# Five edits to a fused two-layer decoder trunk: order of the softmax division, of a weight load, of three scheduled steps, and a weight sum by accumulating transfer

## The chip, the cores and the metric

The kernel runs on one core of a Trainium2 chip. The metric is device microseconds per execution; the kernel before has a median of 2035.91 us in three runs. The engines are TensorE (PE; its weight loads are shown as PEld), VectorE (DVE), ScalarE (ACT), GpSimd (POOL) and SyncE (SP), which here only issues transfers.

## The reference

A trunk of two layers on 256 tokens of width 2048, float32. Layer 0 mixes by gated linear attention (4 heads, chunks of 64 tokens), layer 1 by sliding-window attention with a sink per head (32 query heads, 4 key/value heads, window 128). Each layer ends with a squared-ReLU MLP of width 8192.

```
u = rmsnorm(h, norm_mix[layer])
h = h + gla_mixer(u, ...)            # layer 0: gates from rank-16 product glr @ w_g2
k_band, v_band = shared_kv(h, ...)   # once, after layer 0
h = h + swa_sink_mixer(u, ...)       # layer 1
h = h + sqrelu_mlp(rmsnorm(h, norm_mlp[layer]), w1, w2)
```

In the attention the scores are masked, a softmax with the sink as a further column is taken (`p = softmax(concat([s, sink]))[..., :-1]`), and `o = p @ v`.

## The kernel before

Every float32 weight is read once from HBM in blocks of 512 x 512 (1 MB, tile `ws`, three buffers) and split by `halve`: ScalarE casts it to a high part `wh` (line 114), VectorE subtracts to get the low part `wl` (line 115), in two halves of 128 x 1024 each. The operands are split likewise, and each product is high x high, high x low and low x high. TensorE accumulates in eight banks: two "tp" (transposes), two "ms" and four "acc".

**What sets the order.** Each engine's list is fixed when the kernel is built. Work beside the main products is put off by `later(n, fn)`, due n ticks on, a tick being a quarter or half of a product's matmuls. `high_priority` lets the loads and splits (`WPRI`) and a few small steps (`QPRI`) be taken earlier in an engine's list than where they stand in the code; `issue_after` puts an instruction behind another one. SP issues the weight loads in order, each when its buffer is free.

**Start.** `first_piece` (lines 383, 401, 402) loads x and the first weight in four steps c = 0 to 3, each in six transfers of 256 KB. `glr` (lines 512, 517, 518) then makes the gates' rank from one 1 MB load.

**Gated attention.** `levels(hp, n)` schedules, for a pair of heads hp, the diagonal gram after 4 ticks (lines 601 to 614 in `diag`), and seven levels of decay grams, the first after n ticks and one each two ticks; `CS` is 14. Each level's operands are made by VectorE, GpSimd and ScalarE (lines 584 to 590, tile `mlev`, two buffers), its grams go to an "ms" bank.

**Residual.** `add_to` adds a finished 512-wide column block c to the stream (line 847) and schedules `operands`, which transposes it back (line 831) and scales it for the next product (lines 339, 340). `last` is 2 in both residuals that have room for Strassen-like products, and c = 3 is finished first there.

**MLP, second weight.** `seven` multiplies 1024 x 1024 blocks with seven products (a Strassen-like scheme), for each quarter g of the hidden width and each half n of the output. `product("A", 0, x)` takes a block `x` from the stream; `more(x, 0, 1)` adds a second block to it in SBUF by an accumulating transfer, issued by POOL (line 1004); `y`'s second block `b12` is loaded to `ws` and added by VectorE (line 1088, 128 x 2048). The summed `y` is used by `product("C", 6, y)`, the summed `x` by `product("D", 4, x)`.

**Sliding-window attention.** For each of four head groups g, beside the query product of the next group, `attend` schedules for the two token blocks t: scores and softmax (`a`), `divide` (lines 1291 to 1293), `masked` and `weighted`; `ATT` gives the ticks of t = 0 and t = 1, so that t = 1 goes first in each. `masked` transposes the divided weights for two halves f (line 1302) into "tp" banks; for t = 1 VectorE multiplies them by two masks into `po` and `pv` (line 1310), for t = 0 ScalarE copies them (line 1305). `weighted` multiplies by the values (vv), 64 columns for each f, f = 0 to partitions 0 to 63 of one "ms" bank and f = 1 to 64 to 127.

Of the kernel before, what the change touches and what calls it, by code (L numbers as in the profile page):

```python
# [8 lines left out]
F32 = mybir.dt.float32  # L9
# [7 lines left out]
P = 128  # L17
# [3 lines left out]
KT = D // P  # L21
# [12 lines left out]
WS = 3  # L34
WHL = 4
WPRI = 60
QPRI = 100
LV = 2
WARM = 11
CS = 14  # L40
# [9 lines left out]
def yoco_kernel(ctx: ExitStack, tc: tile.TileContext, x, norms, mlp_w1, mlp_w2, a_w_in, w_glr, w_gate, a_g_o, a_w_o,  # L50
                kv_w_k, kv_w_v, kv_g_k, b_w_q, b_g_q, b_sinks, b_w_o, out):
    nc = tc.nc
# [4 lines left out]
    wp = ctx.enter_context(tc.tile_pool(name="wp", bufs=2))  # L57
# [14 lines left out]
    def later(n, fn):  # L72
        due.setdefault(now[0] + n, []).append(fn)
# [141 lines left out]
    class Seven:  # L215
# [16 lines left out]
        def load(self, i, j):  # L232
            ws = wp.tile([P, 4, C], F32, name="ws", tag="ws", bufs=WS)
            with tc.high_priority(offset=WPRI):
                nc.sync.dma_start(out=ws, in_=self.block(i, j))
            return ws
# [42 lines left out]
        def run(self, after, order="1 21 3 7 31 e 5 20 30 6 2 4"):  # L279

            for step in order.split():
                if len(step) == 2:
                    i, j = int(step[0]), int(step[1])
                    self.plain(i, j, *("EF" if j else "AC"))
                else:
                    (self.ef if step == "e" else getattr(self, "p" + step))(after)
# [178 lines left out]
    def rstd_x():  # L465
        for c in range(NC4):
            later(2 + c // 2, lambda c=c: square_x(c))
        later(5, sum_x)
        later(9, norm_x)
        later(10, lambda: along(rb, rstd))  # L470
        later(10, lambda: nc.scalar.mul(out=rbq, in_=rb, mul=DK ** -0.5))
# [29 lines left out]
    def load_gate():  # L501
# [2 lines left out]
        nc.scalar.copy(out=wgh, in_=wg)  # L504
        nc.vector.tensor_sub(out=wgl, in0=wg, in1=wgh.bitcast(F32))

    def glr(acc, n):


        ws = wp.tile([P, KT, P], F32, name="ws", tag="ws", bufs=WS)  # L510
        with tc.high_priority(offset=WPRI):
            nc.sync.dma_start(out=ws, in_=w_glr.rearrange("(k p) n -> p k n", p=P))
        for j in range(2):
            js = slice(8 * j, 8 * j + 8)
            wh = wp.tile([P, 8, P], F32R, name="wh", tag="wh", bufs=WHL)
            with tc.high_priority(offset=WPRI):
                nc.scalar.copy(out=wh, in_=ws[:, js])
                nc.vector.tensor_sub(out=wh[:, :, 64:96], in0=ws[:, js, 64:96], in1=wh.bitcast(F32)[:, :, 64:96])  # L518
            for k in range(8):
                kt = 8 * j + k  # L520
                mm(acc.rearrange("p u t -> p (u t)"), wh[:, k],
                   act0[kt // 4][2][:, kt % 4].rearrange("p u t -> p (u t)"), kt == 0, kt == KT - 1)
                if kt % 4 == 3:
                    tick()

        def evac():
            z = g2.tile([P, T], F32, name="z", tag="og")
            nc.scalar.copy(out=z, in_=acc[:, 1])
            nc.vector.tensor_add(out=z, in0=acc[:, 0], in1=z)
            nc.vector.tensor_mul(out=z, in0=z, in1=rb)  # L530
            nc.gpsimd.memset(z[96:128], 1.0)
            nc.scalar.copy(out=zin, in_=z)
            nc.vector.tensor_sub(out=zin[32:64], in0=z[32:64], in1=zin.bitcast(F32)[32:64])

        later(n, evac)
# [115 lines left out]
    def levels(hp, n):  # L651
        later(4, lambda: diag(hp))
        for i, s in enumerate(LEVELS):
            later(n + 2 * i, lambda s=s: level(s, hp))
        later(n + 2 * len(LEVELS), lambda: cross(hp))

    run = gemm_k(0, first=first_piece)
    for c in range(NC4):
        if c == NC4 - 1:
            rstd_x()  # L660
        run(c)
    later(3, load_gate)
    glr(bank([P, 2, T], "tp"), 5)
# [3 lines left out]
    for c2 in range(4):  # L667
        later(CS + c2, lambda c2=c2: cumsum(c2))
    go_all(gemm_q(0))
    levels(0, CS - 6)  # L670
    go_all(gemm_k(1))
    go_all(gemm_q(1))
    levels(1, 1)
# [161 lines left out]
    def operands(acts, gains, c, b):  # L835
        tp = back(c, b)
        for a, g in zip(acts, gains):
            if b == 0:
                a[c] = new_act()
            for j in range(2):  # L840
                kt = 2 * b + j
                scaled(a[c], kt, tp[:, j], g[:, c * 4 + kt:c * 4 + kt + 1])

    def add_to(c, acts, gains, sq, r, last=NC4 - 1):

        def evac(t, acc):
            nc.vector.tensor_add(out=xs[c][:, t], in0=acc, in1=xs[c][:, t])
            if not gains:
                return
            junk = sm.tile([P, C], F32, name="junk", tag="junk", bufs=1)  # L850
            nc.scalar.activation(out=junk, in_=xs[c][:, t], func=AF.Square, accum_out=sq[:, t, c:c + 1])
            if t == 0:
                for b in range(2):
                    later(1 + b, lambda b=b: operands(acts, gains, c, b))
                if c == last:
                    later(1, lambda: rstd_of(r, sq))
        return evac
# [81 lines left out]
    def mlp(w1, w2, act, r, gains):  # L939
# [46 lines left out]
        def seven(w, n, op, us, g, acts, gains, sq, nr):  # L986
# [9 lines left out]
            def load(pool, tag, bufs, i, j):  # L996
                ws = pool.tile([P, 4, C], F32, name=tag, tag=tag, bufs=bufs)
                with tc.high_priority(offset=WPRI):
                    nc.sync.dma_start(out=ws, in_=block(i, j).rearrange("(k p) n -> p k n", p=P))
                return ws  # L1000

            def more(ws, i, j):
                with tc.high_priority(offset=WPRI):
                    nc.gpsimd.dma_start(out=ws, in_=block(i, j).rearrange("(k p) n -> p k n", p=P), accum_op=ALU.add)  # L1004
# [9 lines left out]
            def product(b, o, ws):  # L1014
                p, st = use(b)
                halves = halve(ws)
                for k in range(4):
                    wh, wl = halves[k]
                    mm(p, op[o][:, 0, k], wh, st and k == 0, False, skip_group_check=True)
                    mm(p, op[o][:, 0, k], wl, False, False, skip_group_check=True)  # L1020
                    mm(p, op[o][:, 1, k], wh, False, k == 3, skip_group_check=True)
                tick()
                return p
# [43 lines left out]
                    later(1, lambda: rstd_of(nr, sq))  # L1067


            x = load(mp, "wx", 2, 0, 0)  # L1070
            p = product("A", 0, x)
            more(x, 0, 1)
            if g == 0:
                nc.scalar.mul(out=v, in_=p, mul=-1.0)
            else:
                sub(v, p)
            plain(2, 1, "E", "F")
            y = load(mp, "wy", 1, 1, 1)
            product("E", 2, y)
            plain(3, 1, "E", "F")  # L1080
            add(x12, banks["E"])
            add(x22, banks["F"])
            p = product("D", 4, x)
            more(x, 1, 1)
            add(x21, p)
            b12 = load(wp, "ws", WS, 0, 1)
            with tc.high_priority(offset=WPRI):
                nc.vector.tensor_add(out=y, in0=y, in1=b12)
            sub(x22, product("C", 6, y))
            for i in (2, 3):  # L1090
                plain(i, 0, "A", "C", i == 2)
# [101 lines left out]
    def rows(m, n):  # L1193
        return m.rearrange("p (o n) -> p o n", o=1).broadcast_to([P, n, P])
# [90 lines left out]
        nc.scalar.activation(out=es, in_=es, func=AF.Exp)  # L1285
        return es, su, rd

    def divide(sc, st):
        es, su, rd = st
        with tc.high_priority(offset=QPRI):  # L1290
            nc.vector.tensor_add(out=rd, in0=su, in1=es)
            nc.vector.reciprocal(out=rd, in_=rd)
            nc.vector.tensor_mul(out=sc, in0=sc, in1=rd.rearrange("p (b o) -> p b o", o=1).broadcast_to([P, 8, P]))  # L1293

    def masked(t, sc):

        scp = sc.rearrange("p (a f) n -> p f a n", f=2)
        pos = []
        for f in range(2):
            tp = bank([P, 4, P], "tp")  # L1300
            for p in range(4):
                nc.tensor.transpose(out=tp[:, p, :], in_=scp[:, f, p], identity=ident)
            po = s2.tile([P, 4, P], F32, name="po", tag="po")
            if t == 0:
                nc.scalar.copy(out=po, in_=tp)
                pos.append(((po, 0),))
            else:
                pv = s2.tile([P, 4, P], F32, name="pv", tag="pv")
                for o, m in ((po, ownT), (pv, prevT)):
                    nc.vector.tensor_mul(out=o, in0=tp, in1=rows(m, 4))  # L1310
                pos.append(((po, 1), (pv, 0)))
        return pos

# [12 lines left out]

    def attend(g):

        sc, sums, pos = {}, {}, {}

        def a(t):
            sc[t] = s2.tile([P, 8, P], F32, name="sc", tag="sc")
            scores(g, t, sc[t])
            sums[t] = softmax(g, t, sc[t])

        def b(t):
            pos[t] = masked(t, sc[t])

        for t in range(NT):
            steps = (lambda t=t: a(t), lambda t=t: divide(sc[t], sums[t]), lambda t=t: b(t),  # L1340
                     lambda t=t: weighted(g, t, pos[t]))
            for n, step in zip(ATT, steps):
                later(n[t], step)
# [56 lines left out]
```

## Time and profile before

| | us |
|---|---|
| median of three runs (lowest, highest) | 2035.91 (2034.97, 2035.98) |
| profiled execution, own time | 2036.59 |
| its span | 2034.9 |
| TensorE busy | 2023.3 (99%) |
| VectorE busy | 1546.8 (76%) |
| ScalarE busy | 1202.9 (59%) |
| GpSimd busy | 161.4 (8%) |
| mean granted TensorE clock | 1.00 |

A line of the timeline gives the start (us from the span's start), the duration, engine, source line, operation, output and inputs with shapes, how many such instructions in a row, and in brackets how long the engine had been idle and what ended that. A line of the waits gives the waiting engine's output and line, what it waited for, the total, the count and the longest, in us. Matmuls are pipelined: a record is longer than the distance to the next one, and busy time counts overlapping records once.

### The profile page before, as it was taken

To read this page: it belongs to the slowest core of one execution; us is meant where nothing else is said; L and a number is where in the kernel's file an instruction comes from. 1 tells how busy PE (TensorE), PEld (TensorE's weight loads), DVE (VectorE), ACT (ScalarE), POOL (GpSimd) and SP (SyncE) were. 2 spreads that over 40 slices of the span, in tenths; PEclk is the share of its full clock that TensorE was granted. 3 is DMA by queue.
4 is the path that set the end of the run, shared out by engine and by line. 5 is a ranking of instruction groups with operands and counts; after the bars stand their busy time and mean duration, and the time that the engine had idled before them with its cause. 6 is when DMAs were issued, how large, how long until landed. Compare 5 with 4: busy or idle time off the path is not lost.

```text
span 2034.9 us, 26993 instructions
## 1 busy us (share of the span) xinstructions
PE 2023.3 (99%) x10578; PEld 1716.3 (84%) x10578; DVE 1546.8 (76%) x1796; ACT 1202.9 (59%) x1638; POOL 161.4 (8%) x175
## 2 busy tenths in 40 slices
PE   9999999999999999999999999999999999999999
PEld 9988888888888888888887877788888888888887
DVE  6698787867866876786798676876876786787777
ACT  6746666656555655555566677655655555555555
POOL 2151110000000000000001121000000000000000
PEclk9999999999999999999999999999999999999999
DMA  8445876676965785776666543775785786687575
GB/s 287 160 140 179 224 207 207 188 255 179 267 229 190 225 267 186 213 242 228 186 207 188 166 145 123 200 258 186 227 264 191 200 255 218 188 255 230 186 224 148
DMA packets 219280, 423.15 MB, mean 208 GB/s; under 512 B 7328, under 2 KB 17840, under 8 KB 219152
## 3 DMA queue, kind: packets, MB, share of 16 engines
q1 hardware_dynamic: 194224, 376.59, 54.3%
q0 software_dynamic: 21568, 42.81, 12.2%
q10 hardware_dynamic: 3360, 2.01, 0.3%
q8 instruction: 83, 1.36, 0.3%
q14 instruction: 45, 0.37, 0.1%
HBM read 419.29 MB, written 2.10 MB: 207 GB/s over the span
## 4 chain that ended last, share of the span: by engine, by line
PE 91%; DVE 4%; ACT 2%; DMA 1%; issue 1%; POOL 0%; SPq 0%; ACTq 0%; DVEq 0%; POOLq 0%
PE acc L81 58%; PE ms L81 22%; PE tp L81 10%; DVE wl L115 1%; ACT sc L1283 1%; DMA ws<-in_a_w_in_dram 1%; DMA wx<-in_mlp_w_dram 1%; PE tp L831 0%; ACT wh L114 0%; DVE sc L1293 0%; PE tp L1215 0%; DVE st L1277 0%; DVE act L340 0%; PE tp L701 0%; DVE po L1310 0%
## 5 line engine op out<-in xcount | busy, mean ns | idle before, releaser
L115 DVE TENSOR_TENSOR wl<-ws,wh 128x1024 fp32r<-128x1024 f32 x600 | 737.7, 1238 | 277.9 <-ACT wh L114 274.6
L114 ACT CAST wh<-ws 128x1024 fp32r<-128x1024 f32 x600 | 629.0, 1052 | 448.9 <-PE acc L81 285.9
L81 PE MATMUL acc<-wh,act 128*128 128x512 f32 x1696 | 544.5, 394 | 0.5 <-DVE xs L1042 0.3
L81 PE MATMUL acc<-act,wh 128*128 128x512 f32 (+1 forms) x1536 | 453.7, 359 | 0.0
L81 PEld LDWEIGHTS acc<-wh,act 128*128 128x128 f32 x1696 | 317.5, 188 | 69.0 <-issue 2.0
L81 PE MATMUL acc<-act,wl 128*128 128x256 f32 x1280 | 355.1, 279 | 0.1
L81 PE MATMUL acc<-wl,act 128*128 128x512 f32 x848 | 330.2, 390 | 0.0
L81 PEld LDWEIGHTS acc<-act,wh 128*128 128x128 f32 x1536 | 272.6, 189 | 43.5
L115 DVE TENSOR_TENSOR wl<-wx,wh 128x1024 fp32r<-128x1024 f32 x160 | 193.5, 1222 | 87.6 <-ACT wh L114 85.2
L114 ACT CAST wh<-wx 128x1024 fp32r<-128x1024 f32 x160 | 167.9, 1054 | 143.4 <-PE acc L81 81.1
L81 PEld LDWEIGHTS acc<-act,wl 128*128 128x128 f32 x1280 | 241.3, 189 | 1.6 <-DVE wl L402 0.3
L81 PE MATMUL tp<-act,wh 128*128 128x512 f32 x528 | 204.6, 392 | 0.8 <-DVE wh L518 0.8
L81 PE MATMUL ms<-act,wh 128*128 128x512 f32 x512 | 202.0, 394 | 0.0
L81 PEld LDWEIGHTS acc<-wl,act 128*128 128x128 f32 x848 | 159.4, 188 | 32.8 <-issue 1.4
L81 PE MATMUL ms<-wh,act 128*128 128x512 f32 x512 | 163.4, 390 | 0.0
L81 PE MATMUL ms<-act,wl 128*128 128x256 f32 x512 | 143.4, 280 | 0.0
L1004 POOL DMA_DIRECT2D wx<-in_mlp_w_dram x32 | 41.2, 1288 | 1268.2 <-DVE wl L115 1252.5
L81 PE MATMUL tp<-act,wl 128*128 128x256 f32 x512 | 140.7, 275 | 0.0
L81 PE MATMUL acc<-wh,ops 128*128 128x512 f32 (+1 forms) x392 | 123.6, 386 | 0.3 <-ACT wh L114 0.3
L81 PE MATMUL acc<-wh,op 128*128 128x512 f32 x384 | 123.4, 389 | 0.0
L81 PEld LDWEIGHTS tp<-act,wh 128*128 128x128 f32 x528 | 99.1, 188 | 24.3 <-DVE wh L518 1.0
L81 PEld LDWEIGHTS ms<-act,wh 128*128 128x128 f32 x512 | 95.7, 187 | 21.6
(278 smaller groups left out, 2556.2 us busy)
## 6 DMA issues: line engine op xcount, KB each, us to landing
ws<-in_mlp_w_dram SPq DMA_DIRECT2D x224, 1024.0 KB, 5.3
ws<-in_a_w_in_dram SPq DMA_DIRECT2D x42, 1024.0 KB, 5.0
wx<-in_mlp_w_dram POOLq DMA_DIRECT2D x32, 1024.0 KB, 9.2
wx<-in_mlp_w_dram SPq DMA_DIRECT2D x16, 1024.0 KB, 5.1
wy<-in_mlp_w_dram SPq DMA_DIRECT2D x16, 1024.0 KB, 7.8
ws<-in_b_w_q_dram SPq DMA_DIRECT2D x16, 1024.0 KB, 5.0
ws<-in_a_w_o_dram SPq DMA_DIRECT2D x15, 1024.0 KB, 5.1
ws<-in_b_w_o_dram SPq DMA_DIRECT2D x15, 1024.0 KB, 5.0
```

The lines of the kernel that those rows point to most:

```text
L81: nc.tensor.matmul(o, lhsT=l, rhs=r, start=start, stop=stop, **kw)
L114: nc.scalar.copy(out=wh[:, js, :o], in_=w)
L115: nc.vector.tensor_sub(out=wl[:, ks, :o], in0=w, in1=wh.bitcast(F32)[:, js, :o])
L1004: nc.gpsimd.dma_start(out=ws, in_=block(i, j).rearrange("(k p) n -> p k n", p=P), accum_op=ALU.add)
L1283: nc.scalar.activation(out=sc[:, h], in_=sc[:, h], func=AF.Exp, bias=nmx[:, h:h + 1], scale=f[:, h:h + 1], accum_out=su[:, h:h + 1])
```

## The change

Five edits. (1) The load of the gates' rank is issued ahead of the pieces of c = 3. (2) The levels of the first pair of heads start one tick earlier, `CS - 7`. (3) The operands of column block c = `last` are made one tick later. (4) In the last quarter (g = 3) of the first MLP the product with `y` stands first, and `y`'s second block is added by an accumulating transfer, not by a load and a VectorE addition. (5) `masked` of t = 1 collects its mask instructions in `ins`; a later `divide` of the same head group, that of t = 0, is put behind the last of them.

```diff
+    wglr = []
+    def load_glr():
+        wglr.append(wp.tile([P, KT, P], F32, name="ws", tag="ws", bufs=WS))
+        with tc.high_priority(offset=WPRI):
+            with tc.issue_after(tail[nc.sync].ins):
+                tail[nc.sync] = nc.sync.dma_start(out=wglr[0], in_=w_glr.rearrange("(k p) n -> p k n", p=P))
     def glr(acc, n):
-        ws = wp.tile([P, KT, P], F32, name="ws", tag="ws", bufs=WS)
-        with tc.high_priority(offset=WPRI):
-            nc.sync.dma_start(out=ws, in_=w_glr.rearrange("(k p) n -> p k n", p=P))
+        ws = wglr[0]
...
             rstd_x()
+            load_glr()
         run(c)
...
-    levels(0, CS - 6)
+    levels(0, CS - 7)
...
-                    later(1 + b, lambda b=b: operands(acts, gains, c, b))
+                    later(1 + (c == last) + b, lambda b=b: operands(acts, gains, c, b))
...
+            def one():
+                x = load(mp, "wx", 2, 0, 0)
+                p = product("A", 0, x)
+                more(x, 0, 1)
+                if g == 0:
+                    nc.scalar.mul(out=v, in_=p, mul=-1.0)
+                else:
+                    sub(v, p)
+                return x
+            def three():
+                y = load(mp, "wy", 1, 1, 1)
+                product("E", 2, y)
+                return y
+            late = g == 3 and gains
+            if late:
+                y = three()
+                more(y, 0, 1)
+                x = one()
+                plain(2, 1, "E", "F")
             else:
+                x = one()
+                plain(2, 1, "E", "F")
+                y = three()
             plain(3, 1, "E", "F")
...
-            b12 = load(wp, "ws", WS, 0, 1)
-            with tc.high_priority(offset=WPRI):
-                nc.vector.tensor_add(out=y, in0=y, in1=b12)
+            if not late:
+                b12 = load(wp, "ws", WS, 0, 1)
+                with tc.high_priority(offset=WPRI):
+                    nc.vector.tensor_add(out=y, in0=y, in1=b12)
             sub(x22, product("C", 6, y))
...
-    def divide(sc, st):
+    def divide(sc, st, ins):
         es, su, rd = st
-        with tc.high_priority(offset=QPRI):
+        with ExitStack() as order:
+            order.enter_context(tc.high_priority(offset=QPRI))
+            if ins:
+                order.enter_context(tc.issue_after(ins[-1].ins))
             nc.vector.tensor_add(out=rd, in0=su, in1=es)
...
                 for o, m in ((po, ownT), (pv, prevT)):
-                    nc.vector.tensor_mul(out=o, in0=tp, in1=rows(m, 4))
+                    ins.append(nc.vector.tensor_mul(out=o, in0=tp, in1=rows(m, 4)))
```

TensorE's list at the division, first head group, before: the transposes of t = 0 (`sc`, eight), then the four products of t = 1 with the values.

```order
L1302 MATMUL tp<-ident,sc 128x128 [waits DVE_49,PE_49,Activation_49]
L1302 MATMUL tp<-ident,sc 128x128 [waits Activation_49] x3
L1302 MATMUL tp<-ident,sc 128x128 [waits DVE_49,PE_49]
L1302 MATMUL tp<-ident,sc 128x128 x2
L1302 MATMUL tp<-ident,sc 128x128 [waits Activation_49]
L81 MATMUL ms<-po,vv 64x512
L81 MATMUL ms<-pv,vv 64x512
L81 MATMUL ms<-po,vv 64x512
L81 MATMUL ms<-pv,vv 64x512
```

The same place in the changed kernel:

```order
L81 MATMUL ms<-po,vv 64x512 [waits DVE_49]
L81 MATMUL ms<-pv,vv 64x512 [waits DVE_49]
L1329 MATMUL tp<-ident,sc 128x128 [waits DVE_49,PE_49,Activation_49]
L1329 MATMUL tp<-ident,sc 128x128 [waits Activation_49] x3
L1329 MATMUL tp<-ident,sc 128x128 [waits PE_49]
L1329 MATMUL tp<-ident,sc 128x128 x2
L1329 MATMUL tp<-ident,sc 128x128 [waits Activation_49]
L81 MATMUL ms<-po,vv 64x512
L81 MATMUL ms<-pv,vv 64x512
```

The products of f = 0 have moved ahead of the transposes, those of f = 1 have stayed behind; groups two and three read the same, and in the fourth three products stand ahead and one behind. VectorE's list at this place, before (`st` are the softmax's sums, L1206 reduces the next query's squares, L115 splits a weight):

```order
L1291 TENSOR_TENSOR st<-st 128x8 [waits Activation_49]
L1310 TENSOR_TENSOR po<-tp,ownT 128x512 [waits PE_49]
L1292 RECIPROCAL st<-st 128x8 [waits DVE_49]
L1310 TENSOR_TENSOR pv<-tp,prevT 128x512
L1293 TENSOR_TENSOR sc<-sc,st 128x1024 [waits DVE_49]
L1310 TENSOR_TENSOR po<-tp,ownT 128x512 [waits PE_49]
L1310 TENSOR_TENSOR pv<-tp,prevT 128x512
L1206 TENSOR_REDUCE hv<-hsq 128x8 [waits Activation_49]
L115 TENSOR_TENSOR wl<-ws,wh 128x1024 [waits DMAHW4_49]
```

And in the changed kernel:

```order
L1337 TENSOR_TENSOR po<-tp,ownT 128x512 [waits PE_49]
L1337 TENSOR_TENSOR pv<-tp,prevT 128x512
L1337 TENSOR_TENSOR po<-tp,ownT 128x512 [waits PE_49]
L1337 TENSOR_TENSOR pv<-tp,prevT 128x512
L1318 TENSOR_TENSOR st<-st 128x8 [waits Activation_49]
L1230 TENSOR_REDUCE hv<-hsq 128x8 [waits Activation_49]
L1319 RECIPROCAL st<-st 128x8 [waits DVE_49]
L115 TENSOR_TENSOR wl<-ws,wh 128x1024 [waits DMAHW2_49]
L1320 TENSOR_TENSOR sc<-sc,st 128x1024 [waits DVE_49]
```

The four masks stand together, and the division (L1320) comes behind them, a reduction and a weight's low part. In SP's list at the start the gates' rank has moved ahead of the six transfers of c = 3:

```order
L513 DMA ws<-in_w_glr_dram 128x16x128
L383 DMA xt<-in_x_dram 128x2x256
L383 DMA ws<-in_a_w_in_dram 128x512 x2
L383 DMA xt<-in_x_dram 128x2x256
L383 DMA ws<-in_a_w_in_dram 128x512 x2
```

Before, the row of `w_glr` followed these four; the rest of that part of the list reads the same.

More of the change, by code (lines that the diff above doesn't have):

```diff
@@ L1067, in done @@
                     later(1, lambda: rstd_of(nr, sq))
[L1070 to L1074, printed above, removed]
-            else:
[L1076 to L1079, printed above, removed]
+            def one():
[17 more added lines that the diff above has]
+                plain(2, 1, "E", "F")
+            else:
+                x = one()
+                plain(2, 1, "E", "F")
+                y = three()
             plain(3, 1, "E", "F")
@@ L1293, in divide, with masked @@
             nc.vector.tensor_mul(out=sc, in0=sc, in1=rd.rearrange("p (b o) -> p b o", o=1).broadcast_to([P, 8, P]))
-    def masked(t, sc):
+    def masked(t, sc, ins):
         scp = sc.rearrange("p (a f) n -> p f a n", f=2)
@@ L1327, in attend @@
     def attend(g):
-        sc, sums, pos = {}, {}, {}
+        sc, sums, pos, ins = {}, {}, {}, []
         def a(t):
@@ L1336, in b @@
         def b(t):
-            pos[t] = masked(t, sc[t])
+            pos[t] = masked(t, sc[t], ins)
         for t in range(NT):
-            steps = (lambda t=t: a(t), lambda t=t: divide(sc[t], sums[t]), lambda t=t: b(t),
+            steps = (lambda t=t: a(t), lambda t=t: divide(sc[t], sums[t], ins), lambda t=t: b(t),
                      lambda t=t: weighted(g, t, pos[t]))
```

## The prediction

> **What bounds the kernel now.** I read the page's busy table first, then the waits of TensorE (PE), then stretches of its timeline around each wait.
>
> ```profile
> span 2034.9 us, 26993 instructions
> PE 2023.3 (99%) x10578; PEld 1716.3 (84%) x10578; DVE 1546.8 (76%) x1796; ACT 1202.9 (59%) x1638; POOL 161.4 (8%) x175
> ```
>
> TensorE is busy for 2023.3 of 2034.9 us, so only 11.6 us of idle time are there to be won, warm-up and tail included. The change takes out no matmul. It can win at most the waits it reaches, and every microsecond by which it lengthens TensorE's own work adds to the end in full. The waits, by what ended them (total, times, longest):
>
> ```profile
> PE tp L1302 <- DVE pv L1310: 2.6, 4, 1.6
> PE ms L81 <- DVE AT L614: 0.9, 1, 0.9
> PE tp L81 <- DVE wh L518: 0.8, 1, 0.8
> PE acc L81 <- DVE wl L115: 0.7, 1, 0.7
> PE tp L831 <- DVE xs L847: 0.5, 1, 0.5
> PE ms L1050 <- DVE xs L1041: 0.4, 1, 0.4
> PE acc L81 <- DVE xs L1042: 0.3, 1, 0.3
> ```
>
> L1302 are the transposes of attention weights, four waits, one for each head group. L518 is the gates' rank, L614 the level grams' diagonal, L115 and L1042 the last quarter of the first MLP. The tail (L1050, L1041) is not touched. All that the five edits reach comes to about 6 us, 0.3% of the time. About 0.2%, 4 us, is what a measurement of this kernel can tell from no change.
>
> **The division tied behind the masks.** This is the largest term and I cost it first. The stretch of the first head group, TensorE:
>
> ```profile
> 1176.68 0.60 PE L1302 MATMUL tp<-ident,sc 128*128 128x128 f32 x4
> 1177.52 0.63 PE L1302 MATMUL tp<-ident,sc 128*128 128x128 f32 x4 [0.24 <-DVE pv L1310]
> 1178.07 1.08 PE L81 MATMUL ms<-po,vv 128*64 128x512 f32 x4
> 1178.98 1.03 PE L81 MATMUL ms<-pv,vv 128*64 128x512 f32 x4
> 1179.95 0.28 PE L1215 MATMUL tp<-identr,qhl 128*128 128x128 f32 x1
> ```
>
> The eight transposes of block t = 0 are 0.11 us apart; between the two fours there are 0.40 us of wait (0.24 shown idle, the rest is the modelled end). The four products of weights and values of block t = 1 (po and pv, for f = 0 and f = 1) take 1178.07 to 1179.95, 1.88 us, and are eight records. From the first transpose to the end it is 3.27 us. What one such record costs is told by the groups that keep shapes apart (busy us, mean ns):
>
> ```profile
> L81 PE MATMUL ms<-v,AT 128*128 128x512 f32 x24 | 11.6, 592 | 0.0
> L81 PE MATMUL ms<-po,vv 128*64 128x512 f32 x32 | 8.7, 618 | 0.0
> L81 PE MATMUL ms<-pv,vv 128*64 128x512 f32 x16 | 4.1, 592 | 0.0
> ```
>
> One record lasts as long on 64 columns as on 128 (592 to 618 ns), but 24 records on 128 columns keep TensorE busy for 11.6 us, 0.48 each, and 48 on 64 columns for 12.8, 0.27 each. So the 64-column ones run two at a time: f = 0 writes the lower half of the partitions, f = 1 the upper half, and the two halves of the array work side by side. The Trainium skill ("TensorEngine Tiling (Array Packing)", Tiling Modes) says that different tiles can execute weight loads and matmuls in parallel, and that a change of tiling mode drains the engine; the trace agrees with the first (0.27 against 0.48 us), and the second speaks against more switches between 64 and 128 columns.
>
> The order of the changed kernel, shown above, puts f = 0's two products ahead of the eight transposes and leaves f = 1's two behind. A transpose uses all 128 columns, so no half can run beside it: each pair is alone on its half of the array. Two products are four records one after another, 4 x 0.47 = 1.88 us, as long as all four took together. So TensorE's work grows by 1.88 us in each of the first three groups. In the fourth three products go ahead and one stays behind: 0.94 more.
>
> Then the wait. The transposes need the divided weights. VectorE (DVE) in the same stretch:
>
> ```profile
> 1173.62 0.16 DVE L1291 TENSOR_TENSOR st<-st 128x8 f32<-128x8 f32 x1
> 1173.69 0.69 DVE L1310 TENSOR_TENSOR po<-tp,ownT 128x512 f32<-128x512 f32 x1
> 1174.29 0.19 DVE L1292 RECIPROCAL st<-st 128x8 f32<-128x8 f32 x1
> 1174.40 0.64 DVE L1310 TENSOR_TENSOR pv<-tp,prevT 128x512 f32<-128x512 f32 x1
> 1174.96 1.22 DVE L1293 TENSOR_TENSOR sc<-sc,st 128x1024 f32<-128x1024 f32 x1
> 1176.69 0.68 DVE L1310 TENSOR_TENSOR pv<-tp,prevT 128x512 f32<-128x512 f32 x1
> 1177.29 0.68 DVE L1206 TENSOR_REDUCE hv<-hsq 128x8 f32<-128x512 f32 x1
> 1177.88 1.22 DVE L115 TENSOR_TENSOR wl<-ws,wh 128x1024 fp32r<-128x1024 f32 x1
> 1179.01 0.17 DVE L346 TENSOR_SCALAR hv<-hv 128x8 f32<-128x8 f32 x1
> ```
>
> Start to start, a mask takes 0.60, the reduction 0.59, a weight's low part 1.13, the reciprocal 0.11, the sum 0.07. In the new order the four masks come first: 1173.62 + 4 x 0.60 = 1176.0. Then the sum, the reduction, the reciprocal and, moved ahead of the division, a weight's low part: 1176.0 + 0.07 + 0.59 + 0.11 + 1.13 = 1177.9; the division's 1.22 ends at 1179.15, against 1176.2 now. The masks end 1.3 us earlier, so the wait on a free bank goes, but the weights come 3 us later. Today's release takes 0.15 us (the mask ends at 1177.37, the transpose starts at 1177.52), so the transposes start at 1179.3. TensorE is through with f = 0's pair at 1176.68 + 1.88 = 1178.56 and waits 0.74. Altogether 1.88 + 0.74 + 0.88 + 1.88 = 5.38 us in place of 3.27: +2.1 us. The next two groups have the same order and short waits (2.6 less 1.6 for three), so +2.1 each.
>
> The fourth group differs:
>
> ```profile
> 1274.56 0.60 PE L1302 MATMUL tp<-ident,sc 128*128 128x128 f32 x4
> 1276.74 0.63 PE L1302 MATMUL tp<-ident,sc 128*128 128x128 f32 x4 [1.58 <-DVE pv L1310]
> 1279.17 0.50 PE L81 MATMUL acc<-wh,act 128*128 128x512 f32 x1
> ```
>
> 4.61 us today, with a wait of 1.74 (1276.74 less 1274.56 and 0.44). After: three products side by side 1.88, a wait for the division that I put near 1.1 (one low part fewer ahead of the masks' end than today, two operations of 1.13 and 1.22 behind it), transposes 0.88, one product 0.94: 4.8, +0.2. Sum of the edit: 3 x 2.1 + 0.2 = **+6.5 us**. Bounds: if every division is in time, 3 x 1.88 + 0.94 less the waits of today (1.0 + 1.6 shown, with restarts 3.2) is +3.4; if one more low part gets ahead of each division, +11.
>
> **The last quarter of the first MLP.** n = 0 and 1 lose a 2.29 us addition and a 1 MB load each, and gain an accumulating transfer.
>
> ```profile
> 1071.26 0.61 PE L81 MATMUL acc<-wh,op 128*128 128x512 f32 x2
> 1072.56 0.50 PE L81 MATMUL acc<-wl,op 128*128 128x512 f32 x1 [0.69 <-DVE wl L115]
> L1088 DVE TENSOR_TENSOR wy<-wy,ws x16: 2281/2286/2293, 504.9 to 1994.6; 128x2048 f32<-128x2048 f32 x16
> 1060.00:1080.00 20.00, 19.31 (x89) 15.35 (x87) 19.50 (x26) 12.56 (x19) 1.28 (x1) 1.00 0.77 218
> ```
>
> From 1060 to 1080 VectorE is busy for 19.50 of 20 us (third of the busy columns), and TensorE waits for the low part of the summed weight: 1071.49 + 0.23 = 1071.72 was due, 1072.56 came, 0.84. Without the addition VectorE gains 2.29 us, more than that, and the 0.3 (about 0.5 with its restart) of L1042 behind it goes too: **-1.3 us**. The bounds are -1.4 and, where the new transfer is late, +3. It is the longer of the two kinds:
>
> ```profile
> 1006.63 1.28 POOL L1004 DMA_DIRECT2D wx<-in_mlp_w_dram  x1 [112.22 <-DVE wl L115]
> 1024.24 1.28 POOL L1004 DMA_DIRECT2D wx<-in_mlp_w_dram  x1 [16.33 <-DVE wl L115]
> wx<-in_mlp_w_dram POOLq DMA_DIRECT2D x32, 1024.0 KB, 9.2
> ```
>
> POOL issues the first block's sum at 1006.63, and at 1024.24 the sum's last cast is done. The casts of two halves take about 2.5 us, so they start near 1021.7. In the new order the second weight is first: its sum goes out near 1006.6 and the first block's one to two products later (2.73 us each), 1009.4 to 1012. With 9.2 us from issue to landing it is there at 1018.6 to 1021.2, 0.5 us early at worst, and the queue is shared with the other sum. By the Trainium skill ("DMA: Bandwidth & Descriptors", Anatomy of one DMA) one software-issued transfer takes 2 us and its bytes at 436 GB/s, an estimate of 4.4 us here, by which nothing could be late; the trace's 9.2 us decides.
>
> **The gates' rank fetched ahead.**
>
> ```profile
> 29.97 0.28 PE L81 MATMUL acc<-act,wh 128*128 128x256 f32 x1
> 31.08 2.12 PE L81 MATMUL tp<-act,wh 128*128 128x512 f32 x8 [0.83 <-DVE wh L518]
> 22.14 0.60 ACT L401 CAST wh<-ws 128x512 fp32r<-128x512 f32 x1
> DMA packets 3979, 6.95 MB, mean 347 GB/s; under 512 B 268, under 2 KB 1199, under 8 KB 3976
> ```
>
> TensorE waits 0.99 us (30.09 due, 31.08 came). The 1 MB load moves ahead of the six pieces of c = 3; at the 390 to 400 GB/s of that stretch's full slices (347 over the 20 us with its quiet end) it puts them 2.7 us back. c = 3's first cast was at 22.14, so 24.8 to 25.4, while its 48 matmuls, 0.12 us apart, were due from 30.09 - 5.76 = 24.33: 1.1 us of wait at c = 3 for the 0.99 taken away. **+0.1 us**, between -1 (a cast less delayed) and +1 (low parts late too).
>
> **Levels a tick earlier** put two heads' grams into the same ticks, with two banks and two buffers; the 0.88 us wait on L614's copies (0.9 above) may go or come twice: -0.9 to +0.9, **0** taken. **Operands a tick later** move the transposes of c = 2 alone, behind eight more matmul rows; no wait of today stands there (L831's 0.5 is at c = 3, whose order is the same): **0**, plus or minus 0.3.
>
> **Sum.** +6.5 - 1.3 + 0.1 = +5.3 us on the profiled execution's own 2036.59, 2041.9. That execution was 0.68 above the median 2035.91, so 2041.2 is forecast.
>
> **The rivals.**
> *The pair costs half.* If a lone pair took 0.94 us, the work would be unchanged. For it: 0.47 us per product is what the stretch shows. Against it: the record's length is the same at 64 and 128 columns. Then a group is 0.94 + 1.68 (to 1179.3) + 0.88 + 0.94 = 4.44, +1.2, the fourth about -0.3: +3.3 - 1.2 = +2.1, 2038.0, not slower. The same side is reached if the divisions come in time: +3.4 - 1.2, 2038.1. It decides wherever the edit costs below 5.2 us. 25%.
> *Every touched wait goes.* 3.2 + 1.3 + 1.0 + 0.9 = 6.4 off, 2029.5. It needs the transposes not to wait at all, and the longer work not to be: 7%.
> *The first block's sum is late.* Each n waits up to 1.5 us at the product after it, decided by a landing above 9.7 us from issue: 2041.2 + 3 = 2044.2. For it: half of the present ones take over 9.2. 12%.
> *The forecast:* 52%, with 2039 to 2043.5 as its own range, about a tenth of it below the bound of slower. The last 4% are mixtures between the first two, no change.
>
> Slower is 0.12 + 0.46 = 0.58; within 0.2% 0.25 + 0.06 + 0.04 = 0.35; faster 0.07. The range 2035.5 to 2044.0 takes in the first rival and leaves out the second and most of the third.
>
> **What would show it.** Right: in each of three groups po and pv records 0.43 to 0.48 us apart instead of in pairs, TensorE's busy time up by about 6 us, waits of the transposes on the division of 0.6 to 1.1 us; the waits at 1072 and 1081 gone; one near 24.5 us in place of the one at 31; wx and wy sums landed ahead of their casts. Wrong: records of f = 0 still in pairs, or transposes that start with no wait. Slower with TensorE's busy time unchanged would mean that the loss is a wait I have not named.

## The result, and the profile after

| us | before | changed |
|---|---|---|
| median of six runs (lowest, highest) | 2035.95 (2034.97, 2036.43) | 2053.27 (2050.95, 2054.93) |
| span of the profiled execution | 2034.9 | 2052.5 |
| TensorE busy | 2023.3 | 2032.8 |
| mean granted TensorE clock | 1.000 | 0.997 |

The ratio is 1.0085 (95% interval 1.0072 to 1.0098): 17.3 us slower. A loss was forecast, but 5.3 us of it. The busy times of the changed kernel's page:

```profile
PE 2032.8 (99%) x10578; PEld 1719.4 (84%) x10578; DVE 1544.0 (75%) x1794; ACT 1203.2 (59%) x1638; POOL 167.5 (8%) x177
```

VectorE is 2.8 us less busy than before and TensorE 9.5 us more, with no matmul added. TensorE's waits (total, times, longest):

```profile
PE tp L838 <- DVE act L340: 7.2, 1, 7.2
PE tp L1329 <- DVE hv L346: 1.9, 3, 0.7
PE acc L81 <- ACT wh L401: 1.4, 1, 1.4
PE tp L1329 <- DVE sc L1320: 1.2, 1, 1.2
PE ms L81 <- POOL ones L89: 1.2, 1, 1.2
PE acc L81 <- DVE wl L402: 1.0, 3, 0.3
PE ms L81 <- POOL mlev L592: 0.8, 1, 0.8
```

The waits at L1310, L518 and L115 are gone, as meant. In their place stands one of 7.2 us that before has nowhere, at the transposes (L838, before L831) of the columns that the first MLP has just finished. (L346, which the second row names, is the operation behind the division on VectorE: in the first head group the division ends at 1189.83 and the transposes start at 1189.98.) Both traces have 10578 TensorE records, so the start of the record with the same number, in one and the other, tells where the 17.6 us of span came in:

| stretch (us, changed) | later by | forecast |
|---|---|---|
| 0 to 39, start | +2.05 | +0.1 |
| 39 to 1060, levels, operands of the first residual | +0.5 | 0 |
| 1060 to 1093, last quarter of the first MLP | +8.2 | -1.3 |
| 1180 to 1300, attention, four groups | +2.2, +2.2, +2.1, +0.6 | +2.1, +2.1, +2.1, +0.2 |
| 1300 to the end | -0.3 | 0 |

The large row, in TensorE's timeline of the changed kernel:

```profile
1068.22 0.39 PE L81 MATMUL ms<-wl,act 128*128 128x512 f32 x1
1075.85 1.09 PE L838 MATMUL tp<-ident,xs 128*128 128x128 f32 x4 [7.25 <-DVE act L340]
1076.59 1.20 PE L81 MATMUL ms<-wh,act 128*128 128x512 f32 x2
```

Stretches of 4 us around it (TensorE's busy time, records, granted clock, share of the transfer engines, GB/s):

```profile
1068.00:1072.00 4.00, 0.60 (x3) 0.88 1.03 383
1072.00:1076.00 4.00, 0.15 (x1) 0.50 0.05 19
1076.00:1080.00 4.00, 4.00 (x12) 0.50 0.04 6
1080.00:1084.00 4.00, 4.00 (x16) 0.84 1.07 175
1084.00:1088.00 4.00, 4.00 (x20) 1.00 0.55 101
```

The idle 7.25 us are not the whole price. The clock falls to 0.50 while TensorE is idle and stays there for some 5 us of work after it; in the 4 us from 1076 on, 12 records run where 20 fit at full clock. The stretch lost 9.8 us, 7.4 by the wait and 2.4 by the clock. (1.6 came back between 1081 and 1093, where waits of before are gone.) The Trainium skill ("TensorE: Matmul & The Clock Gate", Part 1) says that the clock halves after an idle window of about 3.4 us and needs as long a busy one to return; the trace agrees in kind, but not in the figures: the clock fell at 1071.0, 2.4 us after the last matmul's end, and was full again at about 1081.2, 5.3 us after the first one.

Who held the operands up shows in ScalarE's timeline:

```profile
1061.68 0.82 ACT L339 ACTIVATE act<-tp,gT 128x256 fp32r<-128x256 f32 x2
1071.25 1.04 ACT L114 CAST wh<-wx 128x1024 fp32r<-128x1024 f32 x1 [8.75 <-DMA wx<-in_mlp_w_dram]
1072.20 0.83 ACT L339 ACTIVATE act<-tp,gT 128x256 fp32r<-128x256 f32 x2
```

The transfers between 1053 and 1072 us show why: rates in 40 slices, the queue of software-issued transfers (packets, MB, share), and issue to landing:

```profile
GB/s 0 0 0 0 0 78 95 99 177 207 207 207 207 211 207 207 211 185 168 185 194 207 211 250 259 229 263 254 267 263 250 285 362 401 392 397 392 405 414 341
q0 software_dynamic: 1056, 2.10, 63.6%
wy<-in_mlp_w_dram POOLq DMA_DIRECT2D x1, 1024.0 KB, 8.8
wx<-in_mlp_w_dram POOLq DMA_DIRECT2D x1, 1024.0 KB, 14.2
```

In the second half (n = 1) y's sum was issued at 1053.53, x's 3.5 us behind it at 1057.00. Accumulating transfers move at 207 GB/s while no ordinary load runs, half of the 400 of the ordinary loads at the end of the row. Two of them, 2.10 MB, need 10 us, so x's sum came through behind y's. That alone would not have made it late: by 1064 the two had moved 1.54 MB, and at 207 GB/s the other 0.56 would have been through at 1066.7 (an estimate), 9.7 us from x's issue. But from about 1064 on ordinary loads share the transfer engines with it, and x's sum landed at 1071.18, 14.2 us from its issue. ScalarE's next instruction was the cast of that sum. It waited 8.75 us, and the scaling of the operands (L339), which needs no transfer, waited behind it; VectorE's half of it waited for ScalarE, the transpose banks stayed full, and TensorE stopped.

### The profile page after: what moved, and what is told of

Its sections match the earlier page's. It is cut to its first block, busy times and chain, and to the rows that moved or that the text cites. A ratio compares the mean times of both kernels' runs of the same rounds, so it can differ in the third digit from the quotient of the medians.

```text
span 2052.5 us, 26981 instructions
## 1 busy us (share of the span) xinstructions
PE 2032.8 (99%) x10578; PEld 1719.4 (84%) x10578; DVE 1544.0 (75%) x1794; ACT 1203.2 (59%) x1638; POOL 167.5 (8%) x177
## 4 chain that ended last, share of the span: by engine, by line
PE 88%; DVE 4%; DMA 3%; issue 2%; ACT 2%; POOL 0%; ACTq 0%; SPq 0%; POOLq 0%; DVEq 0%
PE acc L81 56%; PE ms L81 21%; PE tp L81 10%; DVE wl L115 1%; DMA wx<-in_b_w_o_dram 1%; ACT sc L1307 1%; DMA wx<-in_mlp_w_dram 1%; DMA ws<-in_a_w_in_dram 1%; DMA xt<-in_x_dram 0%; ACT wh L114 0%; PE tp L838 0%; DVE st L1301 0%; DVE sc L1320 0%; PE tp L1239 0%; PE tp L708 0%
## 5 line engine op out<-in xcount | busy, mean ns | idle before, releaser
L115 DVE TENSOR_TENSOR wl<-ws,wh 128x1024 fp32r<-128x1024 f32 x600 | 739.0, 1240 | 281.9 <-ACT wh L114 279.0
L115 DVE TENSOR_TENSOR wl<-wx,wh 128x1024 fp32r<-128x1024 f32 x160 | 193.4, 1222 | 90.1 <-ACT wh L114 87.5
```

The costliest lines, as they stand in the source:

```text
L115: nc.vector.tensor_sub(out=wl[:, ks, :o], in0=w, in1=wh.bitcast(F32)[:, js, :o])
```

## The experiments

**Each large edit undone.** e1_no_late sets the last quarter back:

```diff
-            late = g == 3 and gains
+            late = False
```

> The changed kernel with the last quarter of the first MLP as before (order, load and addition of y's second block). Theory: the accumulating sum of the first block x lands 14 us after its issue, ScalarE waits for it with the operands' scaling queued behind, TensorE idles 7.25 us and then runs at half clock for about 8 us; all of that, 8.4 us from 1060 to 1090 us, goes: 2053.3 - 8.4 = 2044.9 us, and the clock is 1.00. Rival: the late transfer only shows a shortage made earlier (by the start or the levels), and the wait comes back elsewhere: 2050 or more.

Measured 2044.3 us (2043.82 to 2044.68), ratio 1.0038 (1.0024 to 1.0053), clock 1.00. The theory holds: the edit costs 9.0 us between medians. (The half clock lasted some 5 us of work, not 8.)

e2_no_tie leaves the division where it was:

```diff
-            if ins:
+            if False:
                 order.enter_context(tc.issue_after(ins[-1].ins))
```

> The changed kernel with the division not tied behind the masks. Theory: split pairs of 64-column products and later divisions cost 2.1 us in three head groups and 0.6 in the fourth; all of it goes, 7.0 us: 2046.3 us, and po and pv records come in pairs again. Rival (a lone pair costs half, the loss between 1180 and 1300 us is inherited from the half clock before): 2051 to 2053.

Measured 2046.6 us (2043.48 to 2048.12), ratio 1.0048 (1.0033 to 1.0063). The theory holds: the edit costs 6.7 us. po and pv come in pairs again, and among TensorE's waits the four of before are back, with the long one of 1.6:

```profile
PE tp L838 <- DVE act L340: 8.1, 1, 8.1
PE tp L1329 <- DVE pv L1337: 2.7, 4, 1.6
```

e3_no_glr loads the gates' rank behind c = 3:

```diff
             rstd_x()
-            load_glr()
         run(c)
+    load_glr()
```

> The changed kernel with the gates' rank loaded after the pieces of c = 3, as before. Theory: the start loses 2.0 us by the load ahead (waits at c = 3 of 1.5 and 0.6 and at c = 2 of 0.9, less the 0.99 of the gates' rank): 2051.2 us, with the wait of 0.8 to 1.0 us at 31 us back. Rival (the time at the start varies from run to run with the transfers): no change, 2053.

Measured 2051.91 us (2050.68 to 2052.76), between the two; the ranges overlap with the changed kernel's, so this run does not settle it. Its trace and that of e2_no_tie keep the changed order of the last quarter; that stretch is 7.5 and 9.1 us later in them, where it is 8.2 in the changed kernel.

e4_levels_operands is the kernel before with the levels and the operands alone (the three edits above undone together).

> The kernel before with two edits alone: levels a tick earlier and operands of the last column block a tick later. Theory: by the distances of equal matmuls in the two traces these are worth +0.5 less 0.3 and -0.3: 2035.9 plus or minus 0.5 us, and the three other edits carry all of the 17.3 us (8.4 + 7.0 + 2.0). Rival: the levels collide and cost 1 to 2 us: 2037 to 2038.

Measured 2036.39 us, ratio 1.0001 (0.9991 to 1.0010). The theory holds: nothing that can be measured. In its trace the levels cost 0.5 us between 37 and 152 us, and 0.6 and 0.4 us are won from 1060 to 1093 and from 1310 to 1380 us.

**Why x's sum was late.** e5_order_only keeps y's product first, and takes y's sum from the software queue:

```diff
             if late:
                 y = three()
-                more(y, 0, 1)
                 x = one()
...
-            if not late:
+            if True:
                 b12 = load(wp, "ws", WS, 0, 1)
```

> The changed kernel with y's second block loaded by SP and added by VectorE again, y's product still first and x's sum still by accumulating transfer. Theory: x's sum is late because y's sum is in the same software queue 3.5 us ahead of it and the ordinary loads take their share; with y's sum out of the way x's lands about 9.5 us after its issue, near 1066.5 us, ScalarE waits for it some 4 us at most, the transposes of the operands wait less than 1 us, TensorE keeps its full clock: 2045 to 2047 us. Rival (the ordinary loads alone slow the transfer, or the order alone leaves it too little time): x's sum takes over 12 us, the wait of 5 to 7 us and the half clock stay: 2050 or more.

Measured 2046.96 us in one run. x's sum, issued at 1055.93, landed in 9.17 us, and the clock stayed at 1.00. ScalarE's timeline in this kernel:

```profile
1060.61 0.82 ACT L339 ACTIVATE act<-tp,gT 128x256 fp32r<-128x256 f32 x2
1065.17 1.05 ACT L114 CAST wh<-wx 128x1024 fp32r<-128x1024 f32 x1 [3.75 <-DMA wx<-in_mlp_w_dram]
```

And its largest wait of TensorE:

```profile
PE tp L838 <- DVE act L340: 2.2, 1, 2.2
```

So without the second sum in the queue the 14 us do not come: x's sum is nearly through when the ordinary load starts, near 1063. What those loads add was not tried by itself. But the order alone already costs: the first block's sum is issued one product later and needed at the same place, ScalarE waits 3.75 us for it and TensorE 2.2, where I had expected under 1. In the stretch the order costs 2.3 us, the second sum, with the half clock that follows from it, the other 6.

e6_sum_old_order gives y's sum to the queue in the order of before:

```diff
             late = g == 3 and gains
             if late:
-                y = three()
-                more(y, 0, 1)
                 x = one()
                 plain(2, 1, "E", "F")
+                y = three()
+                more(y, 0, 1)
```

> The kernel before with levels and operands as in e4_levels_operands and with y's sum by an accumulating transfer, issued behind y's product in the order of before (x first, then its sum, two products, y). Theory: the two sums are then 6 to 8 us apart, x's lands before its product as today and y's about 9 us after its issue, just before its casts; the 2.29 us addition is gone, and with it the waits of 0.84 and 0.52 us near 1072 and 1081: 2036.4 - 1.3 = 2035.1 us. Rival (any second sum in this stretch is late): y's sum takes over 12 us, TensorE waits 2 us or more near 1072: 2038 or more.

Measured 2037.54 us, ratio 1.0008 (0.9999 to 1.0018). The sums, 8 us apart, took 9.8 and 9.0 us, as the theory had it, but the gain did not come, and the rival's 12 us did not either. ScalarE's timeline at y's cast:

```profile
1070.30 1.05 ACT L114 CAST wh<-wy 128x1024 fp32r<-128x1024 f32 x1 [3.40 <-DMA wy<-in_mlp_w_dram]
```

And one of TensorE's waits:

```profile
PE acc L81 <- DVE xs L1048: 1.0, 1, 1.0
```

y's sum landed at 1070.2 and ScalarE waited for it, 3.4 us. The wait at 1072 (0.84) is gone; the next one, at L1048 (before L1042), grew from 0.35 to 1.0. The 2.3 us of VectorE that the edit saves are paid by a transfer that lands as late as the addition ended.

**The start.** e7_rank_long_runs reads the gates' rank ahead in one run of 8 KB per partition:

```diff
-    w_glr.rearrange("(k p) n -> p k n", p=P)
+    w_glr.rearrange("(p k) n -> p k n", p=P)
```

> e4_levels_operands with the gates' rank ahead of c = 3 as in the change, but read in one run of 8 KB per partition in place of sixteen of 512 bytes; the rows of that weight then meet other rows of x, so the gates' values differ, the work is the same. Theory: the 2048 short runs fill the queue, so that the next issue on SP is held for 5 to 6 us (until c = 2's last piece has landed) and c = 3's pieces come 3 to 5 us late; with long runs the issue takes under 1 us, c = 3's first piece lands by 23.5 us and its last by 26.6, and the transfers have no dip between 20 and 24 us. Rival (the issue waits for the buffer or the lane, not for room in the queue): the issue is held as long as before.

SP's timeline in the changed kernel (issue time, duration):

```profile
14.19 0.83 SPq L513 DMA_DIRECT2D ws<-in_w_glr_dram  x1
15.07 6.31 SPq L383 DMA_DIRECT2D xt<-in_x_dram  x1
21.49 0.88 SPq L383 DMA_DIRECT2D ws<-in_a_w_in_dram  x2
```

And in this kernel:

```profile
14.12 0.33 SPq L513 DMA_DIRECT2D ws<-in_w_glr_dram  x1
14.73 0.38 SPq L383 DMA_DIRECT2D xt<-in_x_dram  x1
16.43 1.40 SPq L383 DMA_DIRECT2D ws<-in_a_w_in_dram  x2
```

Measured 2036.11 us in one run. The theory holds: with runs of 512 bytes the next issue is held for 6.31 us, with long ones 0.38, and c = 3's last piece lands at 26.3 in place of 28.9. The rates between 13 and 24 us, in the changed kernel:

```profile
GB/s 428 384 432 406 413 395 443 428 417 373 380 376 432 391 436 384 387 380 410 372 387 413 365 421 357 387 320 194 112 89 74 30 52 127 48 354 402 410 324 291
```

In this kernel:

```profile
GB/s 365 406 417 402 443 417 384 421 436 406 380 369 451 384 387 387 432 413 454 391 432 462 484 469 365 372 328 376 406 376 421 410 369 391 402 391 398 425 384 399
```

The transfers fall to 30 to 190 GB/s for 2 us where the issue was held, and do not where it was not. TensorE gained little by that: it was 0.36 us behind at 37 us, against 0.42 in the next run.

e10_rank_ahead is e4_levels_operands with the load as the change has it (`load_glr()` ahead of the last piece).

> e4_levels_operands with the gates' rank ahead of c = 3 as in the change. Theory: the issue behind it is held for 5 to 6 us and the transfers dip, but TensorE's wait moves from the gates' rank to c = 3 at nearly the same size: +0.1 to +0.5 us against e4_levels_operands, 2035.7 to 2037 us. Rival (the 2.0 us of the changed kernel's profile are the edit's price): 2038 or more.

Measured 2036.76 us, ratio 1.0004 (0.9995 to 1.0013): no change. The issue is held for 4.88 us here too, but TensorE is only 0.42 us behind at 37 us. The 2 us of the changed kernel's profile aren't the edit's price. With the load ahead as in the change, e1_no_late and e2_no_tie are 0.4 and 0.5 us behind there. Kernels with the load behind c = 3 lose as much now and then: e6_sum_old_order 1.83 and e11_pairs_operands 1.85, e3_no_glr and e4_levels_operands 0.3. The landing of the first transfers varies from execution to execution; why was not looked into.

**The attention.** e9_split_only leaves the division where it was before and parts the products of t = 1: `between` makes the transposes of t = 0 between those of f = 0 and f = 1.

```diff
         for f in range(2):
+            with ExitStack() as order:
+                if f and between:
+                    order.enter_context(tc.issue_after(between(tr)))
```

> e4_levels_operands with the division where it was (not tied), and only TensorE's order changed: the two products of f = 0 ahead of the transposes of t = 0, those of f = 1 behind them. Theory (a lone pair lasts as long as two side by side): in each group 1.9 + 0.9 + 1.9 us from the first product to the end in place of 3.3, waits of the transposes gone: +1.4, +1.3, +1.3 and about 0 in the four groups, 4 us in all. Rival (a lone pair costs half): 0.94 + 0.88 + 0.94, a gain of 0.4 to 0.5 per group, and of 1.6 in the fourth.

Measured 2041.61 us in one run; the four groups are 1.6, 1.4, 1.4 and 0.2 us later, 4.6 in all, and TensorE's busy time is 7.4 us longer than before. The theory holds. The first group in its timeline of TensorE:

```profile
1177.26 1.07 PE L1354 MATMUL ms<-po,vv 128*64 128x512 f32 x2
1178.17 1.02 PE L1354 MATMUL ms<-pv,vv 128*64 128x512 f32 x2
1179.12 1.09 PE L1331 MATMUL tp<-ident,sc 128*128 128x128 f32 x8
1180.14 1.07 PE L1354 MATMUL ms<-po,vv 128*64 128x512 f32 x2
1181.05 1.02 PE L1354 MATMUL ms<-pv,vv 128*64 128x512 f32 x2
1182.01 0.50 PE L81 MATMUL acc<-wh,act 128*128 128x512 f32 x1
```

Two records take 0.91 us, as four do before: 1.9 us for two products. In the changed kernel the grouped view says the same, 8.2 us for the 16 pv records that took 4.1 before:

```profile
L81 PE MATMUL ms<-pv,vv 128*64 128x512 f32 x16 | 8.2, 595 | 0.0
```

So of the 7.0 us of the edit, 4.6 are the split (less the waits that go with it), and 2.4 what the late division adds.

e8_pairs_first ties the multiplication alone, and puts the transposes of t = 0 behind `wmm`, the products of t = 1:

```diff
+        with tc.high_priority(offset=QPRI):
+            nc.vector.tensor_add(out=rd, in0=su, in1=es)
+            nc.vector.reciprocal(out=rd, in_=rd)
+            with ExitStack() as order:
+                if ins:
+                    order.enter_context(tc.issue_after(ins[-1].ins))
...
+                with ExitStack() as order:
+                    if wmm:
+                        order.enter_context(tc.issue_after(wmm[-1].ins))
+                    nc.tensor.transpose(out=tp[:, p, :], in_=scp[:, f, p], identity=ident)
...
-        for t in range(NT):
+        for t in reversed(range(NT)):
```

> e4_levels_operands with two changes in the attention: of the division only the multiplication is tied behind the masks (sum and reciprocal stand before them), and all four products of weights and values of block t = 1 stand ahead of the transposes of t = 0. Theory: the four masks end at 1176.2, the division at 1177.4, before TensorE is through with the four paired products (1176.7 + 1.9 = 1178.6), so no wait is left and nothing is split: the four waits of today go, 3.2 us: 2033.2 us, and the four groups show no wait of the transposes. Rival (what costs is the tie, a later division, and not the split): the transposes wait 1 us in each group as in the changed kernel, 2036 to 2040.

Measured 2033.86 us, ratio 0.9992 (0.9982 to 1.0001). That is 1.7 us under the kernel before in the same rounds, at the edge of the noise. No wait of these transposes is left; the groups gain 0.2, 0.4, 0.4 and 1.6 us, 2.6 of the 3.2 expected. e11_pairs_operands leaves the levels as before:

> The kernel before with two edits: operands of the last column block a tick later, and the attention as in e8_pairs_first (multiplication alone behind the masks, the four products of t = 1 ahead of the transposes of t = 0). Theory: -2.7 for the attention and -0.5 for the operands, without the 0.5 that the earlier levels cost: 3 us under the kernel before, 2032.5 to 2033. Rival: the products ahead delay ScalarE's copies and the next queries, and half comes back: 2034.5.

Measured 2034.01 us (2033.27 to 2035.19) against 2036.08 in the same rounds, ratio 0.9988 (0.9979 to 0.9997): faster than both kernels, 2.1 us below the kernel before. The median lies between the theory and the rival, nearer the rival; but in the trace the attention gains 2.5 us and the two later stretches of e4_levels_operands 0.6 and 0.3, as the theory has it, and what is missing in that execution is its start, 1.85 us late. The first group in its timeline of TensorE, four records side by side again and no wait:

```profile
1178.03 1.09 PE L1351 MATMUL ms<-po,vv 128*64 128x512 f32 x4
1178.93 1.03 PE L1351 MATMUL ms<-pv,vv 128*64 128x512 f32 x4
1179.90 1.09 PE L1331 MATMUL tp<-ident,sc 128*128 128x128 f32 x8
```

Its busy times, TensorE's as before at 2023.4 us and now 100% of the span:

```profile
PE 2023.4 (100%) x10578; PEld 1716.1 (84%) x10578; DVE 1546.5 (76%) x1796; ACT 1203.0 (59%) x1638; POOL 166.6 (8%) x175
```

## Why the prediction was right and wrong

**The attention, +6.5 forecast, 7.0 measured: right by its steps.** The split of the pairs, the later division and the three like groups came as reckoned: 5.4 us were worked out for a group, and it took 5.4 (from 1187.45, where the transposes would have started, to 1192.84). The wait shows as 0.5 to 0.7 us, 0.74 was said. The fourth group waited 1.2 us where 1.1 was put, and lost 0.6. TensorE's busy time grew by 7.2 us in e1_no_late, where about 6 was said. The rival of half cost is refuted by e9_split_only.

**The last quarter, -1.3 forecast, +8.2 measured: the wrong step.** "With 9.2 us from issue to landing it is there at 1018.6 to 1021.2, 0.5 us early at worst, and the queue is shared with the other sum." Three things failed in it. First, the step was worked out for n = 0. There it held: the sums were 5.6 us apart, x's took 9.6, and TensorE lost under 0.1 us. It was then taken for n = 1 as well, where no time was to spare. In the kernel before, x's sum of n = 1 was issued at 1050.97 and took 10.96 us, and its cast on ScalarE already waited for it:

```profile
1062.01 1.06 ACT L114 CAST wh<-wx 128x1024 fp32r<-128x1024 f32 x1 [1.24 <-DMA wx<-in_mlp_w_dram]
```

An issue one product later had to be late there; e5_order_only shows that much alone, a wait of 3.75 us. Second, the landing was taken from the median of 9.2 us, of transfers with no other sum near them. In n = 1 the sums were 3.5 us apart, and x's took 14.2. The queue's own rate would not have told it: by the estimate above x's sum ends at 1066.7, hardly later than the median's 1066.2. What it took was the second sum, which pushed x's back, and the ordinary loads, which then ran beside it; the second sum is shown by e5_order_only, the share of the loads rests on the rates. Third, the price. The third rival named the mechanism and gave it 12% and "up to 1.5 us at the product after it", twice. The price was taken as lateness at the product that reads the sum; it fell on ScalarE's list, on the operands' scaling behind the cast, and was 7.4 us of TensorE's time. What stands behind the waiting cast on ScalarE was not asked. The 2.4 us of half clock behind it were in no term. The saving itself was also over-read: in e6_sum_old_order, which has neither the new order nor the late sum, it is nothing.

**The start, +0.1 forecast, 2.05 in the profile:** about right, as e10_rank_ahead shows (0.4 us later at 37 us, where e4_levels_operands without the edit is 0.3 later; no change in the median). The rest is what the start varies by. That the issue is held for 5 to 6 us wasn't foreseen, so the small sum is in part luck. **Levels and operands, 0 forecast:** right within 0.5 us. In the trace the levels swap the 0.9 of L614 for 0.8 at L592. **The conversion** from the profiled execution to the median was -0.7 forecast and is of no weight.

In sum the direction was right, and of 17.3 us the attention's 7.0 were foreseen; 9.5 of the 12 missing lie in the one step above.

## What to carry to other kernels

When a transfer gets later or a new one goes to its queue, do not take its median landing: add up what the queue then holds, its own rate, and what other loads run beside it. Do it for each place where the edit runs, the tightest above all; a cast that already waits for its transfer before the change has no time to give. Then read down the list of the engine that waits for it: what stands behind the waiting cast, and needs no transfer at all, is what stops the next engine. On an engine that is 99% busy, ask of every reordering whether it parts instructions that run side by side; TensorE's busy time per record in the grouped view, 0.27 against 0.48 us here, told that before any run.

## What the runs showed of the hardware that was not expected

A wait of 7.4 us on TensorE cost 9.8: the granted clock was 0.50 from 2.4 us into it until 5 us of work had passed. A wait of 2.2 us (e5_order_only) left it at 1.00. A load of 1 MB in 512-byte runs holds the next issue on the same engine's queue for 4.9 to 6.3 us, until the loads ahead of it have landed (in the changed kernel the issue ends at 21.38 and the last of them landed at 21.37), and lets the transfers run dry (30 to 190 GB/s for 2 us); the same megabyte in 8 KB runs holds it for 0.38. Accumulating transfers moved 207 GB/s while no ordinary load ran: 0.81 MB between 1058 and 1062 us, but 0.51 MB between 1064 and 1068, when an ordinary load moved 0.51 MB beside them. The queues of the changed kernel (packets, MB, share) in the first of these stretches:

```profile
q0 software_dynamic: 410, 0.81, 111.5%
```

And in the second:

```profile
q0 software_dynamic: 253, 0.51, 69.7%
q1 hardware_dynamic: 251, 0.51, 38.7%
```

The Trainium skill ("DMA: Bandwidth & Descriptors", Queues, rings and completion order) says that each transfer engine goes round the queues that have work; equal shares of 0.51 MB agree.
